# Ten weight blocks of two hybrid layers split by engines instead of by transfers

## The chip, the cores and the metric

The kernel runs on one core of one Trainium2 chip. The metric is the device time of one execution in microseconds. Engines are named as the profile names them: PE (TensorE, with PEld for its weight loads), DVE (VectorE), ACT (ScalarE), POOL (GpSimd) and SP (SyncE, which only issues transfers). Every engine takes its instructions strictly in its own order; an instruction that waits holds up all that stand behind it on that engine.

## The reference, cut to what matters

Two hybrid layers, then one mixer layer with a mixture of experts, over 256 rows of width 1024 in float32. Each layer begins with a norm and one wide product with its input weights; the change touches only how these weights get on the chip in the hybrid layers.

```python
def hybrid_layer(x, norm_g, w_in, conv_w, ...):
    h = rms_norm(x, norm_g)
    z = h @ w_in                        # [256, 1024] @ [1024, 2840]
    (rg_x, rg_gate, q, k_c, v_c, k_s, v_s, k_w, v_w, nsa_gate, br_gate) = jnp.split(z, cuts, axis=-1)
    y_a = rg_lru(causal_depthwise_conv(rg_x, conv_w, conv_b), ...) * jax.nn.silu(rg_gate)
    y_b = nsa(q, k_c, v_c, k_s, v_s, k_w, v_w, br_gate, q_g, k_g, ...) * jax.nn.silu(nsa_gate)
    return x + jnp.concatenate([y_a, y_b], axis=-1) @ w_out

def reference(...):
    for l in range(2):
        x = hybrid_layer(x, norm_g[l], w_in[l], ...)
    return second_block(x, ...)         # mixer layer, then the experts (403 MB of weights)
```

## The kernel before

Products keep float32 accuracy with three passes in a rounded format: each operand is stored as a rounded part `hi` and the rest `lo = src - hi`, and `mm3_steps` (L304) adds hi by hi, lo by hi and hi by lo. So every weight block needs a `hi` and a `lo` before PE can go through its second and third pass.

**Blocks.** The weights of a layer come in blocks of 128 partitions by up to 2048 columns (1 MB). Blocks 0 to 15 belong to hybrid layer 0, 16 to 31 to layer 1, those from 32 on to the mixer. Two blocks make a chunk (half of the 1024 rows each). In a hybrid layer the chunks are, in order: queries (blocks 0, 1), selected and window keys and values (2, 3), compressed keys and gates (4, 5, only 1120 columns each), the recurrent input for the convolution (6, 7), two gates (8 to 11), then the output weights (12 to 15). In layer 1 the same with 16 more. Block i lives, `hi` and `lo` together, in ring room `RING[i % 5]`; a new block can be written there only when PE is done with the block five before it.

**Two ways to split.** For blocks 0 to 3, SP loads the raw float32 block into a room of its own (L254), ACT copies it to `hi` with rounding in four quarters (L277), and POOL and DVE in turn subtract to get the quarters of `lo` (L280). For every other block POOL issues a transfer that rounds into `hi` on the way (L256); when it has landed, ACT writes `-hi` into `lo` (L286, four pieces); then POOL issues two transfers that read the same block again and add it onto `lo` (L291). Such a block is read twice from memory and passes three times through POOL's queue.

**Order.** A scheduler lays out each engine's instructions; the code's order decides what is allocated where. `issue` starts loads one chunk ahead. `step` and `merged` mix the recurrent half (`rg_part`, a generator) with attention. In a layer, PE does the query chunk for both row tiles, the key chunk, the compressed chunk (each as `dense`, whose result the profile calls `mm<-w,hT`), then the convolution's input (`denseT`, `mm<-hT,w`: four groups of 24 products with 256 columns), mixed with attention's transposes (L542, L546), which need the rope of queries and keys on DVE (L532 to L412). The product tiles `mm` have two buffers: PE can't begin a third product before ACT has read the first (L503, L509 and L514, L528 and L529).

**Arena.** All other tiles are ranges of one SBUF tile, the arena, kept by a first-fit allocator (`t`, `region`, `free`). The scheduler makes a writer wait for all earlier users of the same range.

After the mixer come the experts: 192 loads of 2 MB by SP (L1544, L1559) into rooms that PE empties.

Of the kernel before, what the change touches and what calls it, by code (L numbers as in the profile page):

```python
# [36 lines left out]
ARENA = 24512  # L37
BLOCK, NB = 4096, 7
RING = (6, 2, 3, 0, 1)
WS = 2  # L40
AS = 1
HN = 4
# [18 lines left out]
def run_all(steps):  # L61

    while True:
        try:
            next(steps)
        except StopIteration as end:
            return end.value
# [18 lines left out]
class Net:  # L86
# [156 lines left out]
    def issue(self, upto):  # L243

        while self.nload < min(upto, len(self.blocks)):
            name, idx, off, n = self.blocks[self.nload][:4]
            b = self.block(RING[self.nload % 5], "w", F32R, 2)[:, :, :n]
            src = self.A[name][idx][:, off:off + n]
            if self.nload < 4:

                if self.nload % 2 == 0:
                    raw = self.block(5 if self.nload else RING[4], "raw", F32, 2)
                src = raw[:, self.nload % 2, :n]
                self.nc.sync.dma_start(src, self.A[name][idx][:, off:off + n])  # L254
            else:
                self.nc.gpsimd.dma_start(b[:, 0], src)  # L256
            self.loaded.append((b, src))
            self.nload += 1
# [4 lines left out]
    def weights_steps(self, name, k, pin=False):  # L263
# [4 lines left out]
        i = self.ntake  # L268
        b, src = self.loaded[i]
# [1 line left out]
        hi, lo = b[:, 0], b[:, 1]  # L271
        m = hi.shape[-1]
        r = lambda a: a.rearrange("p (k n) -> p k n", k=k)
        if i < 4:
            for q in range(4):
                sl = slice(q * m // 4, (q + 1) * m // 4)
                a = self.S.copy(hi[:, sl], src[:, sl])  # L277
                if pin:
                    self.tc.keep_in_program_order(a)
                (self.V if q % 2 else self.G).tensor_tensor(lo[:, sl], src[:, sl], hi[:, sl].bitcast(F32), OP.subtract)  # L280
                yield 0
            return r(hi), r(lo)
        n = 4 if m > 1024 else 1
        for i in range(n):
# [6 lines left out]
                self.G.dma_start(lo[:, sl], src[:, sl], accum_op=OP.add)  # L291
            yield 0
        return r(hi), r(lo)

    def mm3(self, *a):
        for _ in self.mm3_steps(*a):
# [182 lines left out]
    def hybrid(self, l, w0, then):  # L479
# [6 lines left out]
        keep = set(self.live)  # L486
# [196 lines left out]
        for s in range(10):  # L683
# [28 lines left out]
                        self.split(yt, yB[:, 0, i], yB[:, 1, i], V)  # L712
            step(2 * HD)
        run_all(self.side)
        if then:
            self.norm_start(l + 1)
            keep |= {"xn", "g", "nss"}
        wo = [self.weights("w_out", 2) for i in range(2)]
        w0 = self.chunk(self.blocks[self.ntake][0]) if then else None
        self.out_part(yB, wo, then)  # L720
# [1161 lines left out]
```

## Time and profile before

| what | us |
|---|---|
| median of 3 runs | 1502.34 |
| lowest, highest | 1496.47, 1507.82 |
| profiled execution, its own time | 1497.17 |
| span of the profiled execution, first to last instruction | 1495.5 |
| PE busy in the span | 1204.1 (81%) |
| DVE, ACT, POOL busy | 421.6, 314.4, 149.2 |

The profiled execution took 1.67 us outside its span, and lies 5.2 us below the median. All positions in what follows are microseconds from the start of the span. Layer 0 runs to about 158 us, layer 1 to about 305, the mixer to about 560, the experts to the end. Layer 1's query product begins at 158.45.

### The profile page before, as it was taken

The page shows a single profiled execution, that of the slowest core. Times are in us where ns is not written, and L with a number is a line of the kernel's source. Part 1 is how long each engine was busy: PE and PEld are TensorE (multiplying, and loading weights), DVE is VectorE, ACT ScalarE, POOL GpSimd, SP SyncE. Part 2 cuts the span into 40 slices and gives each one's busy share as a digit, 9 for nine tenths or more (in the row PEclk, how much of TensorE's full clock was granted, in tenths as well). Part 3 has the DMA queues.
Part 4 walks back from the last instruction along what each step waited for, and adds up shares of the span by engine and source line. Part 5 has one row for each costly group of instructions (what it writes and reads, how often), then busy time and mean ns, then how long its engine had stood idle before and what let it go on. Part 6 is the DMA issues. An engine that isn't in the chain of part 4 may idle for free.

```text
span 1495.5 us, 20667 instructions
## 1 busy us (share of the span) xinstructions
PE 1204.1 (81%) x8695; PEld 668.8 (45%) x8695; DVE 421.6 (28%) x1250; ACT 314.4 (21%) x751; POOL 149.2 (10%) x202
## 2 busy tenths in 40 slices
PE   6899889989779998787686786876877868768775
PEld 5777687767657674333132331331322313314311
DVE  5556355636235573110110110110101101101010
ACT  5466457564323321000000000000000000000000
POOL 5222331233213100000000000000000000000000
PEclk9899999989889898898897888997988979888897
DMA  9978998898856479999999999999999999999996
GB/s 332 256 193 189 273 256 228 178 229 207 184 114 171 152 279 365 428 429 426 428 427 428 428 428 428 428 428 428 427 428 428 428 427 427 429 428 427 422 408 231
DMA packets 62149, 510.27 MB, mean 341 GB/s; under 512 B 5708, under 2 KB 5836, under 8 KB 34660
## 3 DMA queue, kind: packets, MB, share of 16 engines
q1 hardware_dynamic: 42180, 418.26, 66.7%
q0 software_dynamic: 19872, 90.65, 25.2%
q8 instruction: 70, 1.15, 0.3%
q14 instruction: 27, 0.22, 0.0%
HBM read 507.83 MB, written 1.05 MB: 340 GB/s over the span
## 4 chain that ended last, share of the span: by engine, by line
PE 37%; DMA 33%; issue 4%; DVE 2%; POOL 2%; ACT 0%; POOLq 0%; DVEq 0%; ACTq 0%
DMA slot<-in_wu 19%; DMA arena<-in_wu 13%; PE sc L1610 10%; PE ot L1641 8%; PE tp L1581 8%; PE mm L304 4%; DMA arena<-in_wd 1%; DMA w<-in_w_in 1%; PE tp L1632 1%; POOL w L291 1%; DVE arena L1628 1%; PE mm L1649 0%; PE ot L1059 0%; PE sc L1376 0%; PE ot L1231 0%
## 5 line engine op out<-in xcount | busy, mean ns | idle before, releaser
L1610 PE MATMUL sc<-slot,arena 128*32 128x512 f32 x1424 | 325.4, 737 | 133.9 <-DMA slot<-in_wu 81.7
L1610 PE MATMUL sc<-arena 128*32 128x512 f32 x624 | 185.9, 733 | 61.2 <-DMA arena<-in_wu 37.6
L1610 PEld LDWEIGHTS sc<-slot,arena 128*32 128x32 f32 x1424 | 69.7, 130 | 308.2 <-issue 121.5
L304 PE MATMUL mm<-hT,w 128*128 128x256 f32 (+1 forms) x936 | 137.8, 301 | 10.9 <-DMA w<-in_w_in 7.2
L304 PEld LDWEIGHTS mm<-hT,w 128*128 128x128 f32 (+1 forms) x936 | 123.3, 200 | 23.9 <-DMA w<-in_w_in 8.4
L1581 PEld LDWEIGHTS tp<-arena 128*128 128x128 f32 x512 | 124.3, 334 | 17.9 <-issue 17.9
L1581 PE MATMUL tp<-arena 128*128 128x128 f32 x512 | 128.5, 406 | 2.4 <-DVE arena L1579 2.4
L1641 PE MATMUL ot<-slot,arena 128*32 128x512 f32 x704 | 124.7, 596 | 2.8 <-DMA slot<-in_wd 2.1
L286 ACT ACTIVATE w<-w 128x512 fp32r<-128x512 f32 (+2 forms) x184 | 99.7, 596 | 73.0 <-DMA w<-in_w_in 45.4
L1610 PEld LDWEIGHTS sc<-arena 128*32 128x32 f32 x624 | 40.5, 130 | 165.9 <-issue 75.9
L304 PE MATMUL mm<-w,hT 128*128 128x512 f32 (+1 forms) x432 | 106.1, 400 | 7.5 <-DVE arena L504 4.5
L304 PEld LDWEIGHTS mm<-w,hT 128*128 128x128 f32 x432 | 79.4, 202 | 24.4 <-issue 6.5
L1627 DVE SCALAR_TENSOR_TENSOR arena<-arena,sc 128x512 f32<-128x512 f32 x16 | 11.0, 688 | 265.8 <-ACT arena L1626 265.8
L1628 DVE SCALAR_TENSOR_TENSOR arena<-arena,sc 128x512 f32<-128x512 f32 x16 | 11.0, 688 | 265.2 <-PE sc L1610 265.2
L1651 DVE TENSOR_TENSOR arena<-arena,mm 128x512 f32<-128x512 f32 x64 | 44.0, 687 | 118.4 <-PE mm L1649 118.4
L1641 PE MATMUL ot<-arena 128*32 128x512 f32 x320 | 71.9, 608 | 3.6 <-DMA arena<-in_wd 3.6
L304 PE MATMUL mm<-w,y 128*128 128x512 f32 x288 | 74.0, 402 | 0.1
L291 POOL DMA_DIRECT2D w<-in_w_in x68 | 61.2, 960 | 119.4 <-ACT w L286 101.9
L1634 ACT COPY arena<-tp 128x512 f32<-128x512 f32 x16 | 9.4, 586 | 302.1 <-PE tp L1632 302.1
L1646 ACT COPY arena<-ot 128x512 f32<-128x512 f32 x32 | 18.8, 586 | 250.5 <-PE ot L1641 250.5
L1649 PE MATMUL mm<-arena 128*128 128x512 f32 x128 | 64.6, 628 | 1.6 <-ACT arena L1646 1.4
L1626 ACT ACTIVATE arena<-sc 128x512 f32<-128x512 f32 x16 | 9.6, 597 | 261.4 <-PE sc L1610 261.4
(386 smaller groups left out, 1226.8 us busy)
## 6 DMA issues: line engine op xcount, KB each, us to landing
slot<-in_wg SPq DMA_DIRECT2D x47, 2048.0 KB, 31.3
slot<-in_wu SPq DMA_DIRECT2D x42, 2048.0 KB, 33.6
slot<-in_wd SPq DMA_DIRECT2D x42, 2048.0 KB, 35.4
arena<-in_wu SPq DMA_DIRECT2D x22, 2048.0 KB, 33.4
arena<-in_wd SPq DMA_DIRECT2D x18, 2048.0 KB, 35.0
arena<-in_wg SPq DMA_DIRECT2D x17, 2048.0 KB, 31.9
w<-in_w_in POOLq DMA_DIRECT2D x28, 1024.0 KB, 7.9
w<-in_w_in POOLq DMA_DIRECT2D x56, 512.0 KB, 8.4
```

Of the source, the lines that this page charges most:

```text
L286: a = self.S.activation(lo[:, sl], hi[:, sl].bitcast(F32), AF.Copy, scale=-1.0)
L291: self.G.dma_start(lo[:, sl], src[:, sl], accum_op=OP.add)
L304: ins = self.T.matmul(out, lhsT=lhs[k][a], rhs=rhs[k][b], start=(first and i == 0 and k == 0), stop=(last and i == 2 and k == n - 1))
L1581: ins = T.matmul(self.rows[k // 4][:, k % 4 * 128:(k % 4 + 1) * 128], lhsT=hv[:, tt, k], rhs=D[:, tt], start=(tt == 0 and k % 4 == 0), sto ...
L1610: T.matmul(dst[32 * j:32 * j + 32], lhsT=XT[:, k, 32 * j:32 * j + 32], rhs=w(j), start=(k == 0), stop=(k == 7))
L1627: V.scalar_tensor_tensor(hid, hid, 1.0, pg, OP.add, OP.mult)
L1628: V.scalar_tensor_tensor(hid, hid, 0.5, pu, OP.mult, OP.mult)
L1632: T.transpose(ps[:, k * 128:(k + 1) * 128], hw[:, k], self.ident)
L1641: T.matmul(py[h][32 * j:32 * j + 32], lhsT=HT[:, k, 32 * j:32 * j + 32], rhs=w(j), start=(k == 0), stop=(k == 3))
L1646: S.copy(Y[:, cs], py[h])
L1649: T.matmul(pc, lhsT=DT[:, tt * 128:(tt + 1) * 128], rhs=Y[:, cs], start=True, stop=True)
L1651: V.tensor_tensor(xs, xs, pc, OP.add)
```

## The change

Blocks 4 to 7 and 16 to 21 (`ENGINES`) are split as blocks 0 to 3 are. Their raw data goes into two rooms in the arena, `raw0` for even blocks and `raw1` for odd ones, 2048 columns each. A room is loaded again when both engines have subtracted from it; `nsplit` counts the blocks split so far and `issue` stops at a block whose room still holds one that isn't. Blocks 8 to 15, 22 to 31 and all of the mixer's stay with the transfers. The tiles of a layer are freed a little earlier in the code, so that the two rooms fit for the next layer's first blocks.

```diff
--- before.py
+++ after.py
@@ -37,6 +37,7 @@
 ARENA = 24512
 BLOCK, NB = 4096, 7
 RING = (6, 2, 3, 0, 1)
+ENGINES = (4, 5, 6, 7, 16, 17, 18, 19, 20, 21)
 WS = 2
 AS = 1
 HN = 4
@@ -244,6 +245,8 @@
 
         while self.nload < min(upto, len(self.blocks)):
             name, idx, off, n = self.blocks[self.nload][:4]
+            if self.nload in ENGINES and self.nload - 2 in ENGINES and self.nload - 2 >= self.nsplit:
+                break
             b = self.block(RING[self.nload % 5], "w", F32R, 2)[:, :, :n]
             src = self.A[name][idx][:, off:off + n]
             if self.nload < 4:
@@ -252,6 +255,12 @@
                     raw = self.block(5 if self.nload else RING[4], "raw", F32, 2)
                 src = raw[:, self.nload % 2, :n]
                 self.nc.sync.dma_start(src, self.A[name][idx][:, off:off + n])
+            elif self.nload in ENGINES:
+
+                name = f"raw{self.nload % 2}"
+                src = (self.view(self.live[name][0], [128, 2048]) if name in self.live else
+                       self.t([128, 2048], name))[:, :n]
+                self.nc.sync.dma_start(src, self.A[self.blocks[self.nload][0]][idx][:, off:off + n])
             else:
                 self.nc.gpsimd.dma_start(b[:, 0], src)
             self.loaded.append((b, src))
@@ -271,7 +280,7 @@
         hi, lo = b[:, 0], b[:, 1]
         m = hi.shape[-1]
         r = lambda a: a.rearrange("p (k n) -> p k n", k=k)
-        if i < 4:
+        if i < 4 or i in ENGINES:
             for q in range(4):
                 sl = slice(q * m // 4, (q + 1) * m // 4)
                 a = self.S.copy(hi[:, sl], src[:, sl])
@@ -279,6 +288,11 @@
                     self.tc.keep_in_program_order(a)
                 (self.V if q % 2 else self.G).tensor_tensor(lo[:, sl], src[:, sl], hi[:, sl].bitcast(F32), OP.subtract)
                 yield 0
+            self.nsplit = i + 1
+            if i in ENGINES:
+                if i + 2 not in ENGINES:
+                    self.free(f"raw{i % 2}")
+                self.issue(self.ntake + 1 + self.ntake % 2)
             return r(hi), r(lo)
         n = 4 if m > 1024 else 1
         for i in range(n):
@@ -291,6 +305,8 @@
                 self.G.dma_start(lo[:, sl], src[:, sl], accum_op=OP.add)
             yield 0
         return r(hi), r(lo)
+
+    nsplit = 0
 
     def mm3(self, *a):
         for _ in self.mm3_steps(*a):
@@ -712,9 +728,10 @@
                         self.split(yt, yB[:, 0, i], yB[:, 1, i], V)
             step(2 * HD)
         run_all(self.side)
+        self.free(*(n for n in list(self.live) if n not in keep))
         if then:
             self.norm_start(l + 1)
-            keep |= {"xn", "g", "nss"}
+            keep |= {"xn", "g", "nss", "raw0", "raw1"}
         wo = [self.weights("w_out", 2) for i in range(2)]
         w0 = self.chunk(self.blocks[self.ntake][0]) if then else None
         self.out_part(yB, wo, then)
```

What moves, by engine. A weight tile is called `w_` and its number in each program; L280 and L277 of before stand as L289 and L286 after, L256, L286 and L291 of before as L265, L300 and L305 after, and L528, L529 (the reads of the compressed chunk's product) as L544, L545.

POOL, from the splits of blocks 2 and 3 on. Before, with blocks 4 and 5 as `w_175` and `w_329`, block 6 as `w_331`, 7 as `w_373`, 8 as `w_375`:

```order
L256 DMA w_175<-in_w_in 128x1120
L280 TENSOR_TENSOR w_74<-raw_75,w_74 128x512 x2
L280 TENSOR_TENSOR w_77<-raw_75,w_77 128x512
L256 DMA w_329<-in_w_in 128x1120
L280 TENSOR_TENSOR w_77<-raw_75,w_77 128x512
L291 DMA w_175<-in_w_in 128x560
L256 DMA w_331<-in_w_in 128x2048
L291 DMA w_175<-in_w_in 128x560
L291 DMA w_329<-in_w_in 128x560 x2
L291 DMA w_331<-in_w_in 128x1024 x2
L256 DMA w_373<-in_w_in 128x2048
L256 DMA w_375<-in_w_in 128x2048
```

After, with blocks 4 and 5 again `w_175` and `w_329`, 6 as `w_339`, 7 as `w_377`, and 8, 9, 10 as `w_379`, `w_455`, `w_457`:

```order
L289 TENSOR_TENSOR w_74<-raw_75,w_74 128x512 x2
L289 TENSOR_TENSOR w_77<-raw_75,w_77 128x512 x2
L289 TENSOR_TENSOR w_175<-arena,w_175 128x280 x2
L289 TENSOR_TENSOR w_329<-arena,w_329 128x280 x2
L265 DMA w_379<-in_w_in 128x2048
L289 TENSOR_TENSOR w_339<-arena,w_339 128x512
L265 DMA w_455<-in_w_in 128x2048
L289 TENSOR_TENSOR w_339<-arena,w_339 128x512
L289 TENSOR_TENSOR w_377<-arena,w_377 128x512 x2
L265 DMA w_457<-in_w_in 128x2048
```

The loads and additions of blocks 4 to 7 are gone from the queue; eight subtractions stand there, and the loads of blocks 8 and 9 stand between and ahead of the subtractions of blocks 6 and 7.

ACT in the same stretch, before; `mm_288` is the key chunk's second product, `mm_346` and `mm_383` are the compressed chunk's two, `w_373` and `w_375` blocks 7 and 8:

```order
L509 ACTIVATE arena<-mm_288 128x256
L514 COPY arena<-mm_288 128x256
L528 COPY arena<-mm_346 128x256
L529 ACTIVATE arena<-mm_346 128x24
L286 ACTIVATE w_373<-w_373 128x512 x4
L528 COPY arena<-mm_383 128x256
L529 ACTIVATE arena<-mm_383 128x24
L286 ACTIVATE w_375<-w_375 128x512 x4
```

And after; `mm_350` and `mm_389` are the compressed chunk's products, `w_339` and `w_377` are blocks 6 and 7, `w_379` and `w_455` blocks 8 and 9:

```order
L530 COPY arena<-mm_288 128x256
L286 CAST w_339<-arena 128x512
L544 COPY arena<-mm_350 128x256
L545 ACTIVATE arena<-mm_350 128x24
L286 CAST w_339<-arena 128x512 x3
L300 ACTIVATE w_379<-w_379 128x512 x2
L544 COPY arena<-mm_389 128x256
L545 ACTIVATE arena<-mm_389 128x24
L286 CAST w_377<-arena 128x512 x4
L300 ACTIVATE w_379<-w_379 128x512 x2
L300 ACTIVATE w_455<-w_455 128x512 x2
L564 COPY arena<-tp_440 128x4x128
```

The read of the second compressed product stood behind block 7's rounding load before; after, it stands behind the one of block 8, and the copies of block 7 stand behind it too.

ACT in layer 1, before; `w_1657` is block 21, `mm_1575` and `mm_1616` are the key chunk's products, `mm_1674` and `mm_1711` the compressed chunk's, `w_1659`, `w_1701` and `w_1703` blocks 22 to 24:

```order
L286 ACTIVATE w_1657<-w_1657 128x280 x3
L509 ACTIVATE arena<-mm_1575 128x256
L286 ACTIVATE w_1657<-w_1657 128x280
L514 COPY arena<-mm_1575 128x256
L286 ACTIVATE w_1659<-w_1659 128x512 x4
L509 ACTIVATE arena<-mm_1616 128x256
L514 COPY arena<-mm_1616 128x256
L528 COPY arena<-mm_1674 128x256
L529 ACTIVATE arena<-mm_1674 128x24
L286 ACTIVATE w_1701<-w_1701 128x512 x4
L528 COPY arena<-mm_1711 128x256
L529 ACTIVATE arena<-mm_1711 128x24
```

And after, with `mm_1591`, `mm_1632`, `mm_1694`, `mm_1731` for the same products and `w_1675`, `w_1721`, `w_1723` for blocks 22 to 24:

```order
L525 ACTIVATE arena<-mm_1591 128x256
L300 ACTIVATE w_1675<-w_1675 128x512 x2
L530 COPY arena<-mm_1591 128x256
L300 ACTIVATE w_1675<-w_1675 128x512 x2
L525 ACTIVATE arena<-mm_1632 128x256
L530 COPY arena<-mm_1632 128x256
L300 ACTIVATE w_1721<-w_1721 128x512
L544 COPY arena<-mm_1694 128x256
L545 ACTIVATE arena<-mm_1694 128x24
L300 ACTIVATE w_1721<-w_1721 128x512 x3
L300 ACTIVATE w_1723<-w_1723 128x512
L544 COPY arena<-mm_1731 128x256
```

The reads of `mm_1694` and `mm_1731` stand behind a piece of block 23 and of block 24 now; before, only the second stood behind such a piece, of block 23.

## Rows read from the trace of the kernel before

**Rows 1.** Windows: busy us (instructions) of PE, PEld, DVE, ACT, POOL; clock, DMA share, GB/s.
```profile
45.00:62.00 17.00, 10.10 (x56) 9.01 (x56) 5.06 (x14) 6.15 (x13) 4.68 (x6) 0.70 0.97 301
62.00:158.40 96.40, 94.84 (x668) 73.85 (x669) 59.77 (x227) 64.40 (x170) 23.31 (x33) 1.00 0.84 201
158.40:207.20 48.80, 40.63 (x188) 33.47 (x187) 16.67 (x50) 19.13 (x43) 16.85 (x22) 0.86 1.04 275
...
560.00:1495.50 935.50, 705.90 (x3819) 276.15 (x3819) 127.66 (x300) 46.14 (x88) 0.58 (x1) 0.85 0.99 416
```

**Rows 2.** Timeline, 18 to 28.5 us: start, duration, engine, line, operation, [idle before].
```profile
19.40 0.78 POOL L256 DMA_DIRECT2D w<-in_w_in  x1 [1.19 <-DVE w L280]
20.19 3.82 POOL L280 TENSOR_TENSOR w<-raw,w 128x512 fp32r<-128x512 f32 x3
...
22.04 4.35 DVE L280 TENSOR_TENSOR w<-raw,w 128x512 fp32r<-128x512 f32 x1 [2.08 <-ACT w L277]
...
27.87 0.94 PE L304 MATMUL mm<-w,hT 128*128 128x512 f32 x3 [2.54 <-DVE arena L504]
```

**Rows 3.** Timeline of PE, 45 to 62 us.
```profile
45.08 0.86 PE L304 MATMUL mm<-hT,w 128*128 128x256 f32 x6
...
51.40 1.22 PE L304 MATMUL mm<-hT,w 128*128 128x256 f32 x4 [1.88 <-ACT arena L529]
55.70 1.01 PE L304 MATMUL mm<-hT,w 128*128 128x256 f32 x3 [3.08 <-DMA w<-in_w_in]
...
57.64 4.21 PE L304 MATMUL mm<-hT,w 128*128 128x256 f32 x24
61.93 0.63 PE L542 MATMUL tp<-arena 128*128 128x128 f32 x4
```

**Rows 4.** Timeline of PE, 163 to 208 us.
```profile
163.41 7.31 PE L304 MATMUL mm<-w,hT 128*128 128x512 f32 x31
172.65 4.14 PE L304 MATMUL mm<-w,hT 128*128 128x512 f32 x10 [1.93 <-DVE arena L504]
...
182.37 13.99 PE L304 MATMUL mm<-w,hT 128*128 128x512 f32 x74 [1.80 <-DMA w<-in_w_in]
...
201.04 1.01 PE L304 MATMUL mm<-hT,w 128*128 128x256 f32 x3 [2.02 <-DMA w<-in_w_in]
...
207.30 0.60 PE L542 MATMUL tp<-arena 128*128 128x128 f32 x4
```

**Rows 5.** Line L291 (accumulating transfers), 168.5 to 171.8 us.
```profile
L291 POOL DMA_DIRECT2D w<-in_w_in x4: 856/875/920, 168.6 to 171.7; - x4
...
DMA to landing us min/median/max: 6.2/8.4/10.5
```

**Rows 6.** Line L254 (raw loads by SP), whole span.
```profile
L254 SPq DMA_DIRECT2D raw<-in_w_in x4: 432/459/478, 2.2 to 3.7; - x4
...
DMA to landing us min/median/max: 7.4/9.4/13.4
```

**Rows 7.** Line L256 (rounding loads), 145 to 146 us: one load.
```profile
DMA to landing us min/median/max: 5.6/5.6/5.6
```

**Rows 8.** Line L256, 40 to 41.4 us: two loads.
```profile
DMA to landing us min/median/max: 8.6/9.6/10.5
```

**Rows 9.** Line L256, 172 to 173.2 us: two loads.
```profile
DMA to landing us min/median/max: 11.4/12.5/13.5
```

**Rows 10.** Timeline of DVE, 50 to 54 us: the rope of the first row tile.
```profile
51.48 0.95 DVE L536 TENSOR_TENSOR arena<-arena 128x768 f32<-128x768 f32 x1
...
53.20 0.36 DVE L412 TENSOR_TENSOR arena<-arena 128x192 f32<-128x192 f32 x1
```

**Rows 11.** Groups by line: shapes xcount | busy us, mean ns | idle before.
```profile
L286 ACT ACTIVATE w<-w 128x512 fp32r<-128x512 f32 (+2 forms) x184 | 99.7, 596 | 73.0 <-DMA w<-in_w_in 45.4 <-issue 17.9 <-DMA w<-in_w_out 9.7
...
L280 POOL TENSOR_TENSOR w<-raw,w 128x512 fp32r<-128x512 f32 x8 | 11.7, 1485 | 2.2 <-ACT w L277 2.2
```

**Rows 12.** Line L280 on DVE, whole span: ns min/median/max, when.
```profile
L280 DVE TENSOR_TENSOR w<-raw,w x8: 677/681/4349, 12.1 to 26.4; 128x512 fp32r<-128x512 f32 x8
```


## The prediction

> **What bounds the kernel now.** I read the windows first [rows 1], to see which stretch has time to give. From 560 us on the transfers are busy 99% of the time at 416 GB/s: the experts are bound by memory, and the change doesn't touch them; they only start earlier if what is ahead of them ends earlier. Between 62 and 158 us PE is busy for 94.8 of 96.4 us at full clock: nothing to gain there, but what is gained ahead of it is carried through. Two windows are different. From 45 to 62 us PE is busy for 10.1 of 17 us, at a granted clock of 0.70; from 158.4 to 207.2 for 40.6 of 48.8 us at 0.86, while the transfers are busy all the time (1.04). These are the beginnings of the two hybrid layers, where the blocks in question are used. What ends PE's waits there is in its timelines: transfers of weights (3.08 us in layer 0; 1.80 and 2.02 us in layer 1), and reads of the product tiles by ACT and DVE that stood behind such a transfer (1.88 and 1.93 us) [rows 3, 4]. So transfers of weights bound these two stretches, directly or through ACT's queue.
>
> **What a block costs the transfers.** Four additions of half a block each were issued from 168.6 to 171.7 us and landed 6.2 to 10.5 us later [rows 5]: from 174.8 to 182.2, so 7.4 us for three more, 2.5 us each. Four raw loads of a whole block, issued from 2.2 to 3.7 us, landed from 9.6 to 17.1 [rows 6]: also 2.5 us each. Half a block that is added takes as long as a whole one that is only loaded. A full block thus goes from 2.5 + 2 x 2.5 = 7.5 us of transfers to 2.5, with one latency in place of two in a row. For six full blocks that is 30 us of transfers less, and four of about half the size save some 11 more. That is no gain by itself; the gain is what PE waits less.
>
> **Part A, the first splits (layer 0, 22 to 28 us).** PE waited 2.54 us for DVE's read of the first product, which stood behind a subtraction that took 4.35 us while POOL subtracted for blocks 2 and 3 [rows 2]. In POOL's queue the load of block 4 stood ahead of these (a wait of 1.19 us, then 0.78 us to issue), that of block 5 between them. Both leave POOL. I take 1.3 us; the bounds are 0 (DVE remains as slow) and 2.5 (the whole wait).
>
> **Part B, layer 0, 45 to 62 us.** From the convolution's first product (45.08) to the transposes of the second row tile (61.93) are 16.85 us, in which PE does 47 products of 256 columns (37 in the rows shown, 10 between them) and 6 transposes. At the 0.86 us for 6 that the first row shows, the products are 6.7 us; transposes at 0.63 for 4 are 0.9 [rows 3]. So 9.2 us are waits and half clock. After the change blocks 6 and 7 come raw, early, and PE has block 6 when it needs it. A new wait stands on ACT: the read of the second compressed product and the copies of block 7 are behind block 8's load. That can be issued when the key chunk is done, about 39 us (it was 40.1 behind other work), and nothing else is then on the queues; the nearest row is a load alone, 5.6 us to landing [rows 7], the far one is 8.6 us [rows 8]. With 5.6 it lands at 44.7; two pieces of ACT (0.6 us each [rows 11]) and the reads end at 46.5; the rope takes 2.1 us [rows 10] plus two of DVE's subtractions between its steps, 1.4, so the first transposes start at 50.0, and the second after these (0.9) and 24 products (3.4), at 54.3. That is 7.6 us earlier. Bounds: 4.6 with the far row, 9.2 if nothing waits. I take 7.
>
> **Part C, layer 1, 158 to 207 us.** From the query product (158.45) to the transposes of the second row tile (207.30) are 48.85 us. The work is 96 products of 512 columns at 7.31/31 = 0.236 us, 22.7; 48 of 280 columns, out of the 74 in 13.99 us (26 of which are wide: 6.1), 7.9; 29 of 256 columns, 4.2; 14 transposes, 2.2 [rows 3, 4]. Sum 37.0, so 11.9 us are lost. After the change blocks 16 to 21 no longer pass POOL's queue of transfers, and the waits for the key chunk go. Late next are blocks 22 and 23, which still do. Block 22's room is free when the query product ends (170.7 [rows 4]); its load stands behind POOL's subtractions for blocks 18 to 20 (six of 1.5 us at most [rows 11], two of them half as long), about 174. Alone it lands in 5.6 us [rows 7], at 179.6; before, it took 11.4 to 13.5 there [rows 9]. After two pieces of ACT its first addition is issued at 181 and lands at 186.5; block 23's load, block 24's, block 22's second addition and block 23's two follow at 2.5 us each: 189, 191.5, 194, 196.5, 199. PE ends the compressed chunk near 190 and waits for them; with 12 products after the last (1.7 us) the second transposes stand at 200.7, and by the order 19 more products are done by then than before (2.7 us). That is 9.3 us. Ahead of the layer the four subtractions for blocks 16 and 17 stand on POOL before the norm's power, which PE's transposes wait for; this may cost 1 us. Bounds: 3 (block 22 lands as late after its issue as before, 5.8 us more) and 11.9. I take 8.
>
> **Hidden parts.** ACT does as many pieces per block as before. DVE gets 20 subtractions, of 0.7 us each in the middle [rows 12]; it was busy for a third of these two windows [rows 1], so I cost them at nothing but the 1.4 us above and 0.5 us in part C. If that cover is missing, the second rival below holds. POOL loses three issues per block and gets two subtractions, an even trade. The two rooms take free ranges of the arena; their loads in layer 1 wait for attention's last readers, 14 us ahead of the query product, and a raw block needs some 5 us and its split 3.
>
> **Sum.** 1.3 + 7 + 8 - 0.5 = 15.8, about 16 us. Against the profiled execution's 1497.2 that is 1481. That execution lies 5.2 us below the median of 1502.3, so the median forecast is 1502.3 - 16 = 1486.
>
> **Rivals.**
> *The wait moves to the blocks that stay with the transfers.* ACT's queue stands still until block 8, and in layer 1 pieces of 22 to 24, have landed, and the reads of PE's product tiles are behind them. For it: the order, and that such a read was already the end of two of PE's waits [rows 3, 4]. Against it: these loads find empty queues now. With the landings of [rows 8, 9], parts A to C give 0 + 4 + 3, less 1: 6 us, a median of 1496.
> *POOL holds DVE.* One subtraction of DVE took 4.35 us while POOL subtracted [rows 2], six times the median of 0.68 [rows 12]; POOL's own mean is 1.5 us [rows 11]. Each of the 20 new POOL subtractions can hold up a DVE step that PE waits for (rope, norm, reads of products) by 1.5 us: 30 us at most, and slower than before by 14, a median of 1516. It decides from where more than 11 of the 20 stand in PE's way. Against it: at least half of the eight took 0.68 us or less, though POOL subtracted in the same stretch [rows 12], and most of the 20 fall where PE works on blocks that are ready. The Trainium skill (SBUF — State Buffer, Who interferes with whom) states the rule behind this: a DVE instruction with two SBUF inputs and a GpSimd instruction that reads SBUF exclude each other, and the later one waits for the whole of the other. By that rule the change puts on two engines that exclude each other what the transfers did beside them; the 4.35 us agree with it.
> *Nothing arrives.* If the experts' stream started by something other than PE's progress, both layers could end earlier at no gain: 1502. Against it: their rooms are freed by PE and by the layers' tiles.
>
> **How the numbers follow.** A measurement of this kernel can tell about 1%, 15 us, from no change. Forecast 0.62, the moved wait 0.22, POOL holding DVE 0.08, nothing arriving 0.08. The forecast's parts run from 10 to 22 us, and some seven tenths of it lie over 15 us: faster 0.45. The rest of it, the moved wait and most of the last case are within 1%: 0.47. Slower: 0.08. The range takes the forecast and the moved wait, with the 4 us by which a median of such runs can be off: 1479 to 1500.
>
> **What the profile after would show.** Right: PE's window that begins with the convolution of layer 0 at a clock over 0.9; the transposes of its second row tile 6 to 9 us earlier; layer 1's another 5 to 9; the key chunk of layer 1 without waits; loads of block 8 and 22 landing in under 7 us; 30 to 40 us less of transfers between 25 and 220 us. Wrong: a wait of ACT for block 8 or 22 of over 5 us with PE idle behind it; subtractions of DVE with a mean over 2 us and PE's waits ended by DVE; or both layers earlier and the first expert product not.

## The result, and the profile after

The changed kernel takes 1490.62 us (median of 11 runs, 1489.62 to 1495.42); the kernel before, on the same chip, 1502.69 (median of 11, 1496.47 to 1507.82). The ratio is 0.993, with a 95% interval of 0.9914 to 0.9946: 12.1 us by the medians, 10.5 by the ratio. The profiled execution after took 1491.46 us, with a span of 1489.8.

The windows of two stretches, with the columns of [rows 1]:

```profile
45.00:62.00 17.00, 14.11 (x93) 12.63 (x94) 14.05 (x32) 12.69 (x28) 8.80 (x9) 0.90 0.81 203
...
158.40:207.20 48.80, 43.14 (x292) 37.49 (x291) 31.66 (x76) 26.65 (x60) 20.15 (x22) 0.93 0.79 208
```

Against [rows 1], PE is busy for 14.1 of 17 us in place of 10.1, the clock rose from 0.70 to 0.90, and the transfers' share fell from 0.97 to 0.81; in layer 1 it is 0.93 in place of 0.86, and 0.79 in place of 1.04. DVE is busy for 14.1 us of these 17, up from 5.1. The timeline of PE after, in layer 0, answers to [rows 2, 3]:

```profile
26.61 17.36 PE L320 MATMUL mm<-w,hT 128*128 128x512 f32 x96 [0.67 <-ACT arena L519]
...
45.37 2.63 PE L320 MATMUL mm<-hT,w 128*128 128x256 f32 x17 [0.70 <-ACT arena L545]
...
49.30 0.38 PE L320 MATMUL mm<-hT,w 128*128 128x256 f32 x1 [0.74 <-POOL w L289]
50.72 0.66 PE L558 MATMUL tp<-arena 128*128 128x128 f32 x4 [1.04 <-DVE arena L428]
...
55.82 0.60 PE L558 MATMUL tp<-arena 128*128 128x128 f32 x4
```

The stretch that began at 27.87 begins at 26.61, and the transposes of the second row tile (61.93) stand at 55.82. No wait for a weight transfer is left; the longest is 1.04 us, for DVE's rope. The same for the end of layer 0 and for layer 1, beside [rows 4]:

```profile
123.53 0.96 PE L320 MATMUL mm<-w,y 128*128 128x512 f32 x3
...
151.51 0.63 PE L364 MATMUL tp<-arena 128*128 128x128 f32 x4 [1.62 <-DVE arena L361]
...
152.89 3.40 PE L320 MATMUL mm<-w,hT 128*128 128x512 f32 x14
...
166.91 17.39 PE L320 MATMUL mm<-w,hT 128*128 128x512 f32 x96 [1.32 <-DVE arena L520]
185.37 0.98 PE L320 MATMUL mm<-hT,w 128*128 128x256 f32 x6 [1.07 <-ACT arena L545]
189.04 4.30 PE L320 MATMUL mm<-hT,w 128*128 128x256 f32 x17 [2.69 <-ACT arena L545]
...
197.22 0.63 PE L558 MATMUL tp<-arena 128*128 128x128 f32 x4
```

Layer 0's first output product starts at 123.53 (before: 130.81), so 7.3 us are in hand. PE then waits for DVE at 151.5 (the norm) and at 166.9 (the read of a product), and at the key chunk, where 172.65 became 166.91, 5.7 are left. The second row tile's transposes of layer 1 come 10.1 us earlier (197.22 against 207.30), ACT being what PE waited for last. The query product, at 158.45 before, begins at 152.89. ACT's timeline shows for what it waited itself:

```profile
184.33 0.63 ACT L300 ACTIVATE w<-w 128x512 fp32r<-128x512 f32 x1 [4.94 <-DMA w<-in_w_in]
184.87 0.35 ACT L544 COPY arena<-mm 128x256 f32<-128x256 f32 x1
...
188.00 0.63 ACT L300 ACTIVATE w<-w 128x512 fp32r<-128x512 f32 x1 [1.13 <-DMA w<-in_w_in]
188.54 0.35 ACT L544 COPY arena<-mm 128x256 f32<-128x256 f32 x1
```

ACT waits 4.94 us for the load of block 23, then 1.13 for block 24's, with a read of a compressed product right behind each. What reaches the end is read at the first product of the experts, after and (second line, a trace of the kernel before) before:

```profile
566.77 3.64 PE L1627 MATMUL sc<-arena 128*32 128x512 f32 x32
```

```profile
575.91 3.64 PE L1610 MATMUL sc<-arena 128*32 128x512 f32 x32
```

The difference is 9.1 us. From there on the two traces run alike: the last output has landed at 1490.98 before and 1481.97 after, 9.0 apart. But the spans differ by 5.7 only, since the end of the program became longer (below, among the surprises).

### The profile page after: what moved, and what is told of

The parts are those of the page before. It is cut to its first block, busy times and chain, and to the rows that moved or that the text cites. A ratio compares the mean times of both kernels' runs of the same rounds, so it can differ in the third digit from the quotient of the medians.

```text
span 1489.8 us, 20684 instructions
## 1 busy us (share of the span) xinstructions
PE 1200.4 (81%) x8695; PEld 669.1 (45%) x8695; DVE 447.1 (30%) x1270; ACT 315.5 (21%) x751; POOL 151.8 (10%) x192
## 4 chain that ended last, share of the span: by engine, by line
PE 45%; DMA 37%; issue 8%; DVE 5%; POOL 3%; ACT 2%; POOLq 0%; ACTq 0%; DVEq 0%; SPq 0%
DMA slot<-in_wu 19%; DMA arena<-in_wu 13%; PE sc L1627 10%; PE ot L1658 8%; PE mm L320 8%; PE tp L1598 8%; DMA w<-in_w_in 3%; POOL w L305 1%; PE sc L705 1%; PE tp L841 1%; DMA arena<-in_wd 1%; PE tp L1649 1%; PE ot L719 1%; DVE arena L1645 1%; ACT w L300 1%
## 5 line engine op out<-in xcount | busy, mean ns | idle before, releaser
L1627 PE MATMUL sc<-arena 128*32 128x512 f32 x624 | 185.4, 727 | 63.3 <-DMA arena<-in_wu 38.4
L300 ACT ACTIVATE w<-w 128x512 fp32r<-128x512 f32 (+1 forms) x144 | 81.0, 612 | 50.9 <-DMA w<-in_w_in 19.7
L1658 PEld LDWEIGHTS ot<-slot,arena 128*32 128x32 f32 x704 | 33.2, 109 | 64.3 <-issue 56.1
## 6 DMA issues: line engine op xcount, KB each, us to landing
arena<-in_wg SPq DMA_DIRECT2D x17, 2048.0 KB, 31.3
```

Source lines behind the costliest of these rows:

```text
L300: a = self.S.activation(lo[:, sl], hi[:, sl].bitcast(F32), AF.Copy, scale=-1.0)
L1627: T.matmul(dst[32 * j:32 * j + 32], lhsT=XT[:, k, 32 * j:32 * j + 32], rhs=w(j), start=(k == 0), stop=(k == 7))
L1658: T.matmul(py[h][32 * j:32 * j + 32], lhsT=HT[:, k, 32 * j:32 * j + 32], rhs=w(j), start=(k == 0), stop=(k == 3))
```

## The experiments

Positions in the traces, in us; "traced" is the profiled execution's own time, the last column the median of the timed runs. Layer 0 (L0) and layer 1 (L1) by the second row tile's first transposes and by the first output product.

| kernel | L0 transposes | L0 output | L1 transposes | L1 output | first expert product | traced | median |
|---|---|---|---|---|---|---|---|
| before | 61.9 | 130.8 | 207.3 | 277.4 | 575.9 | 1497.2 | 1502.7 |
| before_2 | 66.1 | 135.0 | 211.7 | 281.8 | 579.7 | 1499.6 | |
| after | 55.8 | 123.5 | 197.2 | 266.4 | 566.8 | 1491.5 | 1490.6 |
| l0_only | 55.5 | 123.5 | 204.0 | 273.9 | 572.7 | 1494.4 | 1495.9 |
| l1_only | 66.4 | 135.3 | 212.4 | 281.2 | 586.2 | 1506.3 | 1501.7 |
| act_order | 54.2 | 125.9 | 197.5 | 273.9 | 574.6 | 1498.8 | 1497.1 |
| sub_dve | 54.0 | 119.7 | 189.6 | 258.3 | 557.1 | 1481.4 | 1491.5 |
| sub_dve_2 | 53.8 | 119.4 | 187.9 | 256.6 | 559.7 | 1484.6 | 1490.8 |
| sub_dve_3 | 53.7 | 131.4 | 200.6 | 269.3 | 570.1 | 1495.1 | |
| more22 | 54.3 | 125.8 | 199.9 | 279.1 | 585.3 | 1509.9 | 1504.9 |
| more22_dve | 53.9 | 119.6 | 185.1 | 267.1 | 569.4 | 1494.7 | 1499.8 |
| more22_sq | 53.6 | 128.8 | 194.3 | 262.0 | 565.0 | 1487.4 | 1492.5 |
| sub_dve_sq | 54.1 | 129.7 | 198.4 | 267.1 | 572.6 | 1498.0 | 1492.2 |
| eng11 | 53.7 | 130.6 | 200.4 | 269.1 | 571.6 | 1495.8 | 1493.4 |

Measured beside the variants, the kernel before had medians of 1502.2, 1503.2, 1502.9 and 1504.3; each ratio below is against the one beside it.

### Each layer alone: l0_only and l1_only

```diff
-ENGINES = (4, 5, 6, 7, 16, 17, 18, 19, 20, 21)
+ENGINES = (4, 5, 6, 7)                      # l0_only
+ENGINES = (16, 17, 18, 19, 20, 21)          # l1_only
```

> Only blocks 4 to 7 (layer 0) are split by engines; layer 1 goes by transfers as before. Theory (each layer's gain is its own and is carried through): layer 0's first output product stands at about 123.5 us as after the whole change (130.8 before), layer 1's loss of 1.5 us ahead of its key chunk is not there, and the first expert product comes at 575.9 - 7.3 = 568.6, a time 7 us under before. Rival (layer 1's blocks by transfers take the gain of layer 0 back, since their loads wait on PE and queue the same way wherever they start): no more than 3 us, first expert product at 573.

> Only blocks 16 to 21 (layer 1) are split by engines; layer 0 as before. Theory: layer 0's output product stays at 130.8 us, the second row tile's transposes of layer 1 come 4.5 us before the 207.3 of before, and the first expert product at about 573 to 574, 2 to 3 us earlier; both halves add up to the 9.1 us of the whole change. Rival (the two halves need each other: layer 1 gains the 8 us of the prediction by itself): first expert product at 568.

l0_only: ratio 0.9961 (0.9938 to 0.9984), 6.3 us by the medians. l1_only: 0.9984 (0.9965 to 1.0003), 0.4 us by the medians, 2.4 by the ratio, and not clear of zero. Together that is 6.7 to 8.3, against 12.1 or 10.5 for the whole: most of it is layer 0, and the halves add up to the whole only roughly, within these intervals. The trace of l0_only has something of both of its readings:

```profile
123.47 0.96 PE L320 MATMUL mm<-w,y 128*128 128x512 f32 x3 [0.20 <-DVE arena L766]
...
155.83 1.09 PE L364 MATMUL tp<-arena 128*128 128x128 f32 x4 [6.65 <-DVE arena L361]
```

Layer 0's output product stands where it does after the whole change, and then PE waits 6.65 us for the norm ahead of layer 1. By the medians the theory's 7 us is nearly there; against the trace of before at 575.9, the first expert product at 572.7 is the rival's number. The two go together because that trace is one of before's quick executions, which the next run shows. The rival's reason is not what the trace shows. Block 16's load was issued 7.3 us sooner than before (138.35 against 145.61), but took 12.5 us to land where it took 5.6 [rows 7]. Ahead of it stands a transfer of 2 MB by SP, the compression weights of layer 1, which the kernel before issued at 163.06 (the second line is that of block 16's load):

```profile
136.84 0.33 SPq L539 DMA_DIRECT2D arena<-in_w_cmp  x1
...
DMA to landing us min/median/max: 12.5/12.5/12.5
```

That this transfer is what holds the load up is read from the order, and was not tested. In the changed kernel it is issued at 138.63, behind the raw loads of blocks 16 and 17 (136.78).

The trace of l1_only fits neither of its readings: its first expert product is at 586.2, where 573 and 568 were expected. Layer 0's output product is at 135.3, where before_2 below has it too, and not at 130.8. From there to the second transposes of layer 1 it is 77.1 us (before 76.5): 6.6 us are gained from the query product on, but 7.1 lost ahead of it, where PE waits 1.08 and 2.89 us for DVE. Another 6.5 us are lost between layer 1's output product and the experts. This trace is of the slowest of its twelve executions.

### The kernel before, traced again: before_2

> The kernel before, once more, for a second trace. Its times spread from 1495.7 to 1512.1 us, and in two traces in which layer 0 has the same program the load of block 6 took 7.5 and 9.8 us to land. Theory (the spread comes from how soon the transfers of the two layers land): span differences appear before the first expert product, which comes later than 575.9 by what the run is longer, and from there to the last product of PE it is 910 to 911 us as in both traces. Rival (the experts' stream varies): first expert product within 1 us of 575.9, and the difference after it.

The same program came to the second row tile 4.2 us later. The load of block 6 in the two traces, before and before_2:

```profile
L256 POOL DMA_DIRECT2D w<-in_w_in x1: 868/868/868, 29.0 to 29.0; - x1
...
DMA to landing us min/median/max: 7.5/7.5/7.5
```

```profile
L256 POOL DMA_DIRECT2D w<-in_w_in x1: 863/863/863, 28.9 to 28.9; - x1
...
DMA to landing us min/median/max: 9.7/9.7/9.7
```

It lands 2.2 us later after its issue, and the additions behind it follow. The first expert product is 3.8 us later, and from there to PE's last product it is 910.6 and 908.5 us, so the experts give back 2.1. So the theory holds for the larger part: in this pair the layers differ by more than the experts do, though its 910 to 911 us are not met. Against this second trace the changed kernel's first expert product is 12.9 us earlier. The gain of 9.1 us read from the first pair is therefore at the low side of what the medians hold.

### The subtractions off POOL: sub_dve, three times

```diff
-                (self.V if q % 2 else self.G).tensor_tensor(lo[:, sl], src[:, sl], ...)
+                (self.V if q % 2 or i in ENGINES else self.G).tensor_tensor(lo[:, sl], src[:, sl], ...)
```

> The subtractions of blocks 4 to 7 and 16 to 21 all go to DVE, none to POOL: 40 in place of 20 on DVE, and POOL reads no SBUF beside them. Theory (DVE and POOL hold each other up, which is why a DVE subtraction takes 1.37 us in the middle): DVE's subtractions of 512 columns fall to about 0.68 us, DVE's steps of one row of small tiles to 0.2 us, layer 1's loss of 1.5 us ahead of its key chunk goes, and the first expert product comes 2 to 3 us before the changed kernel's 566.8. Rival (twice the subtractions on a busy DVE are the price, 0.68 us each, and the two engines don't hold each other): DVE's subtractions keep 1.3 us and the first expert product is 2 to 4 us later.

> The kernel with all subtractions on DVE, once more: its twelve times spread from 1480 to 1499 us with a median of 1491.5, the same as the changed kernel's 1490.6, though the profiled execution, at 1481.4, had its first expert product 9.7 us earlier. Theory (the profiled one was lucky in its transfers; the others lose in the same waits for blocks 8, 22 and 23): a second trace near 1491 has the same durations of DVE (0.68 us) and loses some 10 us behind transfers in the two layers. Rival (the time is lost in the mixer or the experts' stream): first expert product at 557 again, and a longer rest.

> The kernel with all subtractions on DVE a third time, for a trace of one of its slower executions (12 of 20 were over 1489 us; the two traced ones were at 1481 and 1485). Theory: a trace over 1489 has a stretch of half clock of some 20 us in the attention of one of the layers behind a wait of PE of 2 to 3 us that the fast traces don't have. Rival: such a trace is slower in the mixer or in the experts, or shows longer transfers without a fall of the clock.

The line of DVE's subtractions in layer 1 (ns: min/median/max), in the changed kernel and in sub_dve, first two fences, and of a small step of DVE in the changed kernel's layer 0, third:

```profile
L289 DVE TENSOR_TENSOR w<-arena,w x8: 750/1207/1785, 159.8 to 170.8; 128x512 fp32r<-128x512 f32 x4, 128x280 fp32r<-128x280 f32 x4
```

```profile
L289 DVE TENSOR_TENSOR w<-arena,w x16: 443/566/686, 153.4 to 162.8; 128x512 fp32r<-128x512 f32 x8, 128x280 fp32r<-128x280 f32 x8
```

```profile
L335 DVE TENSOR_SCALAR arena<-arena x2: 173/670/1167, 36.4 to 39.9; 128x12 int32<-128x12 int32 x2
```

With POOL beside it, a DVE subtraction takes up to 1.79 us here (1.98 in layer 0), without POOL never more than 0.69, at twice as many. The step of 128 x 12 elements takes 0.17 us and once 1.17, when it began 0.15 us after a subtraction of POOL did and ended with it. Steps that read one operand from PSUM are not touched: two residual sums (L416, at 142.23 and 145.59) lie wholly beside subtractions of POOL and take 0.69 and 0.67 us, and without POOL in the kernel before the same sums take 0.69. So the theory of the hold is right, and the waits of 1.62 and 1.32 us ahead of layer 1's key chunk are gone. In two traces the first expert product comes 9.7 and 7.1 us ahead of the changed kernel's, far more than the 2 to 3 expected. The scheduler also orders PE's work otherwise here, so not all of that is the hold alone.

And yet the median is the same: ratios 0.9923 (0.99 to 0.9947) and 0.9921 (0.989 to 0.9952), times from 1480 to 1499. The second trace, at 1484.6, is a quick one again and decides nothing between its readings. The third, at 1495.1, shows what one of the slower executions loses. ACT in layer 0, in sub_dve_2 and then in sub_dve_3:

```profile
66.97 0.63 ACT L300 ACTIVATE w<-w 128x512 fp32r<-128x512 f32 x1 [1.42 <-DMA w<-in_w_in]
67.62 0.38 ACT L765 ACTIVATE arena<-mm 128x256 f32<-128x256 f32 x1
67.90 0.25 ACT L630 ACTIVATE arena<-tp 15x128 f32<-15x128 f32 x1
```

```profile
68.44 0.63 ACT L300 ACTIVATE w<-w 128x512 fp32r<-128x512 f32 x1 [2.98 <-DMA w<-in_w_in]
69.10 0.38 ACT L765 ACTIVATE arena<-mm 128x256 f32<-128x256 f32 x1
69.38 0.25 ACT L630 ACTIVATE arena<-tp 15x128 f32<-15x128 f32 x1
```

One load, block 11's, has landed 1.47 us later. The reads behind it on ACT (L765 of a product, L630 of the compressed keys) come 1.48 later, and PE, which waited 0.74 us once in sub_dve_2, waits twice:

```profile
69.99 1.09 PE L320 MATMUL mm<-hT,w 128*128 128x256 f32 x7 [0.75 <-DVE arena L766]
72.39 0.28 PE L641 MATMUL tp<-arena 15*128 15x15 f32 x1 [1.30 <-DVE arena L428]
```

From there the granted clock is at the lower of its two levels, 1.2 GHz, for 24 us. Windows of PE, sub_dve_2 first (busy us, instructions, clock, DMA share, GB/s):

```profile
72.00:96.00 24.00, 24.00 (x163) 1.00 0.76 168
```

```profile
72.00:96.00 24.00, 23.61 (x86) 0.51 0.52 98
96.00:120.00 24.00, 24.00 (x178) 0.99 0.53 145
```

In the same 24 us, with PE busy for all but 0.4 of them, 86 matmuls are done in place of 163. Layer 0's output product is at 131.4 in place of 119.4: 12 us, behind 1.5 us of a transfer. This is the theory of the third trace, with waits of 0.75 and 1.30 us. The mean clock of the timed runs fits it, with some overlap: it is 0.883 to 0.893 in the eight under 1487 and 0.877 to 0.886 in the twelve above.

### Order on ACT: act_order

```diff
+LATE = (23, 24)
...
-            if pin:
+            if pin or self.ntake - 1 in LATE:
                 self.tc.keep_in_program_order(a)
```

> As changed, but ACT reads both compressed products of layer 1 before any negation of blocks 23 and 24. Theory of the wait on ACT (what PE lost in layer 1 is that these reads stood behind the loads of blocks 23 and 24, PE waits of 1.07 and 2.69 us there): second row tile's transposes 3 us before the changed kernel's 197.2, first expert product 2 to 3 us before 566.8. Rival (the blocks themselves come late: PE needs the added halves of 22 and 23, which land from 180.8 to 195.3): PE waits as long, behind transfers instead, within 1 us of 566.8 or later.

Ratio 0.9962 (0.9945 to 0.9979), some 6 us behind the changed kernel by the medians. The time is the rival's. Two rows of PE:

```profile
191.17 2.48 PE L320 MATMUL mm<-hT,w 128*128 128x256 f32 x12 [3.04 <-DMA w<-in_w_in]
...
216.60 1.43 PE L320 MATMUL mm<-hT,w 128*128 128x256 f32 x5 [3.14 <-DMA w<-in_w_in]
```

The wait went from ACT to the transfer (3.04 us), the second transposes stayed (197.5), and since block 24's negations had moved back as well, PE later waited 3.14 us for it. After this second wait the clock stands at 0.50 from 216 to 229 us, and the output product is 7.5 us later than in the changed kernel, 2.4 of them from layer 0 of this trace. Counted from its own key chunk (169.35, against 166.91 in the changed kernel) the second transposes do come 2.1 us sooner, part of the theory's 3 us, and the delay of block 24 loses more. So the order on ACT is not the whole of the loss in layer 1: with the reads freed, PE waits for the landing of block 22's second addition instead. How much of the loss is the order and how much the landing, this run does not separate, since it moved block 24 as well.

### Two more blocks by engines: more22, more22_dve

```diff
-ENGINES = (4, 5, 6, 7, 16, 17, 18, 19, 20, 21)
+ENGINES = (4, 5, 6, 7, 16, 17, 18, 19, 20, 21, 22, 23)
```

> As changed, and blocks 22 and 23 are split by engines too. Theory (what is left in layer 1 is these two blocks' double passage through POOL's queue, directly and through the reads on ACT behind them): the PE waits of 1.07 and 2.69 us at 185 to 189 go, the second row tile's transposes come at about 192 to 193 in place of 197.2, and the time falls by 3 to 4 us. Rival (the wait moves on to blocks 24 and 25, three pieces of which now stand ahead of the second compressed product's read): within 1 us of the changed kernel.

> As the run before it (blocks 22 and 23 by engines too), with all subtractions of these blocks on DVE. Theory (POOL's subtractions hold DVE and the norm's power up, and the transfers that are left wait for nothing then): 2 to 3 us better than with half of them on POOL. Rival (24 more subtractions on DVE cost what the lock costs): the same time.

Both expectations failed. more22: ratio 1.0022 (1.0003 to 1.0041), 14 us behind the changed kernel; more22_dve 0.9983 (0.996 to 1.0005). In more22_dve the second row tile's transposes are at 185.1, 12 us ahead of the changed kernel, as the theory wants, and still the output product comes no earlier (267.1 against 266.4). Its ACT, its PE, and PE's windows:

```profile
200.90 0.63 ACT L300 ACTIVATE w<-w 128x512 fp32r<-128x512 f32 x1 [3.49 <-DMA w<-in_w_in]
201.55 0.27 ACT L630 ACTIVATE arena<-tp 15x128 f32<-15x128 f32 x1
```

```profile
204.62 0.23 PE L641 MATMUL tp<-arena 15*128 15x15 f32 x1 [2.94 <-DVE arena L428]
```

```profile
205.00:229.00 24.00, 23.75 (x87) 0.50 0.57 110
229.00:245.00 16.00, 15.76 (x115) 1.00 0.41 133
```

The wait moved on, not to blocks 24 and 25 but to block 27: ACT stood 3.49 us for its load, the compressed keys' square (L630) behind it, PE without work for 2.94 us, and then 24 us at half clock with PE busy: the 12 us. more22 has the same after a wait of 1.98 us (clock 0.64 from 212 to 240), and its second transposes, at 199.9, are not even early.

### Taking that one wait away: more22_sq, sub_dve_sq, eng11

```diff
-                S.activation(sq[0:15], pcv, AF.Square)
+                V.tensor_copy(sq[0:15], pcv); V.tensor_tensor(sq[0:15], sq[0:15], sq[0:15], OP.mult)
...
+ENGINES = (4, 5, 6, 7, 11, 16, 17, 18, 19, 20, 21)     # eng11: sub_dve and block 11
```

> As the kernel with blocks 22 and 23 by engines and all subtractions on DVE, but the square of the compressed keys' norm is taken by DVE (a copy and a product of 15 x 128) in place of ACT, where it stood behind a negation of block 27 whose load landed 8.8 us after its issue. Theory (that wait on ACT left PE without work for 2.94 us ahead of the compressed keys' transposes, and from there to 229 us the granted clock stood at 0.50; the half clock, not the wait, is the 12 us by which 22 and 23 made things worse): PE's wait there falls under 1 us, the clock from 205 to 230 us is 1.0, the first output product of layer 1 comes at about 255 in place of 267.1, and the median falls by some 10 us to 1488 to 1490. Rival (the attention stretch is slow for another reason, such as the later blocks' transfers): the median stays within 3 us of 1499.8.

> As the kernel with all subtractions on DVE (blocks 22 and 23 by transfers), with the same square on DVE. Its times lie from 1480 to 1499 us, with the mean clock at 0.887 to 0.893 below 1486 and at 0.877 to 0.885 above 1492. Theory (the upper ones are executions in which this wait on ACT behind a block that landed late let the clock fall in the attention stretch): with the square off ACT most times lie at 1480 to 1487, median 1485. Rival (the clock falls at another wait, or the other reads on ACT in that chain, which stay, are enough): the spread and the median of 1491 stay.

> As the kernel with all subtractions on DVE, and block 11 is split by engines too. In its slow trace block 11's load landed at 68.4 us against 67.0 in a fast one; ACT's first negation of it stands ahead of the reads from which DVE and PE go on, PE was idle for 0.75 and 1.30 us in place of 0.74, and from 72 to 96 us the granted clock stood at 0.50. Now no block that comes by transfers stands ahead of these reads. Theory (the late landing, by way of the half clock, is the slow mode of 1490 to 1499 us): layer 0 keeps full clock from 72 to 100 us, its first output product comes at about 119.5 in every trace, and the times lie at 1480 to 1487 with a median of about 1484. Rival (the clock falls in layer 0 whatever is ahead on ACT, or in another place): the median stays at 1490 to 1492 and the spread at 15 us or more.

more22_sq: ratio 0.9937 (0.9914 to 0.9961), 1492.5 in place of 1499.8. In its trace PE waits 0.48 us ahead of the compressed keys' transposes of layer 1, the clock from 200 to 240 us is 1.00, and the way from the transposes to the output product, 82.0 us in more22_dve, is 67.7. So in layer 1 it is as the theory says; the output product itself is at 262.0, not 255, because layer 0 fell to half clock this time (0.57 from 72 to 96 us), and the median is above the 1488 to 1490 expected.

sub_dve_sq: 0.9926 (0.9893 to 0.9958), 1480.9 to 1498.0: the rival. Another read (L765) stays behind block 11's negation, and its trace has 0.57 from 72 to 96 us.

eng11: 0.9897 (0.9865 to 0.993), 1482.8 to 1495.8, median 1493.4: the rival again. What was aimed at is reached and does not help. ACT, then PE, in layer 0:

```profile
65.84 0.39 ACT L765 ACTIVATE arena<-mm 128x256 f32<-128x256 f32 x1 [0.43 <-PE mm L320]
66.23 0.27 ACT L630 ACTIVATE arena<-tp 15x128 f32<-15x128 f32 x1
70.88 1.67 ACT L300 ACTIVATE w<-w 128x512 fp32r<-128x512 f32 x3 [4.38 <-DMA w<-in_w_out]
72.45 0.18 ACT L616 ACTIVATE arena<-tp 128x30 f32<-128x30 f32 x1
```

```profile
69.14 0.23 PE L641 MATMUL tp<-arena 15*128 15x15 f32 x1 [0.42 <-DVE arena L428]
...
73.47 1.09 PE L649 MATMUL tp<-arena 128*128 128x64 f32 x4 [2.04 <-DVE arena L645]
```

L765 and L630 wait for no block now, and PE's wait ahead of the compressed keys is 0.42 us. But the next read in the chain, L616, stands behind block 12's load (4.38 us), PE waits 2.04 us one step later, and from 74 to 92 us the clock is 0.50. None of the variants is shown to be faster than the changed kernel: their intervals overlap with 0.9914 to 0.9946.

## Why the prediction was right

The time of 1490.6 lies in the range of 1479 to 1500, between the forecast (1486) and the first rival (1496); the change was clear, though under 1% (0.7%), where the prediction took 1% as the least that could be told. Point by point:

- **Part A**, 1.3 us: measured 1.26 (27.87 to 26.61).
- **Part B**, 7 us: block 8 was issued at 38.4 and landed at 43.7, where 39 and 44.7 were estimated, and ACT's queue held PE up for only 0.70 us. The second transposes came 6.1 us earlier, 4.85 of them after part A, the output product 7.3, or 6.0 after part A. DVE took 0.7 us of the rest: the first transposes are at 50.7, where 50.0 was worked out with 0.7 us for a subtraction; in sub_dve, where it takes that, they are at 50.0. Between the first and the second transposes the clock took more. The second are at 55.8, where 54.3 was worked out, and the granted clock from 50.5 to 56 us is 0.69; act_order and more22, which split the same blocks of layer 0 and have nearly the same waits there, have 1.00, and the second transposes at 54.2 and 54.3. The 24 products between, in the changed kernel and then in act_order:

```profile
51.44 4.54 PE L320 MATMUL mm<-hT,w 128*128 128x256 f32 x24
```

```profile
51.06 3.11 PE L320 MATMUL mm<-hT,w 128*128 128x256 f32 x24
```

- **Part C**, 8 us, is the term that was mis-sized. From layer 0's output product on, the second transposes gained 2.8 us more and the output product 3.7, of which 1.9 were given back ahead of the experts. Counted as the prediction counted, from the query product (158.45, after 152.89), the second transposes came 4.5 us sooner (48.85 to 44.33) where 6.6 were worked out, and the output product 5.4 (118.96 to 113.52) where the 19 products done ahead were to make it 9.3; 1.7 us had been lost ahead of the query product (7.28 to 5.56). The landings were estimated well: block 22's load came 20.8 us after the query product (21.2 estimated), block 23's 31.3 (30.6), block 23's second addition 42.4 (40.6). So the transposes miss the estimate by about what this last addition is late, and of the 2.7 us for the 19 products 0.9 is seen. Meanwhile ACT waited 4.94 us for block 23, PE 1.07 and 2.69 behind it, and the clock was 0.53 from 189 to 195. That is the first rival's mechanism, at 23 and 24; at 8 and 9 it cost 0.70 us. act_order shows that PE waits for the landing too when the reads are freed.
- **POOL and DVE**: the cost "at nothing but 1.4 and 0.5 us" was too low. Ahead of layer 1's key chunk 1.5 us were lost in place of 1 (7.28 to 5.74), and sub_dve's quick traces are 7 to 10 us ahead. The rule of the Trainium skill (SBUF — State Buffer, Who interferes with whom) agrees with the 1.79 against 0.69 us. The 4.35 us that the prediction counted for it are more than the whole of one subtraction of POOL (up to 1.83 in that trace): that step of DVE began at 22.04 and ended at 26.39, past three subtractions of POOL, the last of them from 24.54 to 25.83. No subtraction of DVE took more than 1.98 in the changed kernel. The price of the second rival was real, but nowhere near 30 us, since PE had ready blocks beside most of it.
- **Nothing arrives**: no; the first expert product follows the layers, though not exactly. From layer 1's output product to it the fourteen traces take 297.9 to 306.2 us, a spread that the prediction put at nothing and that no run here explains.
- **The signs named**: the landings of blocks 8 and 22 (5.3 and 5.1 us) and 33 us less of transfers between 25 and 220 us (a share of 0.93 to 0.76) came; layer 1's transposes another 5 to 9 us earlier did not (4.0).

By the traces the parts sum to 9.1 us at the first expert product (12.9 against before_2) where 16 were forecast, and 3.3 us of it are lost again at the end of the program. The median's 12.1 are more than that pair of traces shows, because the profiled execution of before was 5.5 us under its median. The two profiled executions themselves are 5.7 us apart; that the median falls midway between the forecast and the first rival is in that part luck, which no term of the prediction names. That the transfers taken out also take their spread along (nine of the eleven runs after lie within 1.9 us) fits with before_2, but was not tested by itself, and sub_dve, with the same transfers, spreads over 18 us.

What stays open: where the changed kernel loses against sub_dve between 55.8 and 123.5 us (2 us more) beside the changed order; why the clock fell behind the first transposes of layer 0 in the changed kernel and not in act_order, after nearly the same waits; and why after the wait of 2.69 us in the changed kernel the clock was back at 195 us and after 2.94 us in more22_dve only at 229, with PE busy nearly all the time after both.

## What to carry to other kernels

A split that an engine can do beside its other work can be worth more than a transfer that sums, when the queue is what PE waits for: it was for these ten blocks, and not for 22 and 23 on top of them. Price it with the engines as they share SBUF, here 1.8 us in place of 0.7. Before an order is tuned, look for reads of products that stand behind something that waits for a transfer: when the wait is taken away it moves to the next block that still comes so (23, 27, 11 and 12 here). And cost a wait of PE by what the granted clock does after it, not by its length, and look at several executions, since in one pair of them a landing 1.5 us later stood ahead of a loss of 12 us.

## What the runs showed of the hardware that was not expected

- **A short wait, a long half clock.** PE waits of 0.75 and 1.30, 2.04, 2.94 and 3.14 us were followed by 13 to 24 us at 0.50 to 0.51, in stretches in which PE was busy for over 95% of the time; a single wait of 0.74 us in the same place was followed by full clock. The length alone does not decide: in the trace of more22_sq a wait of 1.23 us in layer 0 was followed by half clock (0.57 from 72 to 96 us), and waits of 1.23 and 0.48 us in layer 1 by full clock.
- **A step of one small operand can wait for POOL as well**: 0.17 us became 1.17 beside a subtraction of POOL. The Trainium skill (SBUF — State Buffer, Who interferes with whom) names tensor_scalar, which this step is, among the operations that can take the shared ports; this one execution of it agrees.
- **The end of the program changes with the transfers POOL issued.** The drain of POOL after the last output, before and after (ns: min/median/max):

```profile
L1879 POOLq DRAIN  x3: 40/103/1822, 1491.8 to 1495.2; - x3
```

```profile
L1896 POOLq DRAIN  x3: 40/103/6272, 1482.6 to 1489.4; - x3
```

1.82 us with 138 transfers of POOL and 6.27 with 108; 3.41 with 126, 2.92 with 120, 6.03 with 105, 5.78 with 102. It is the same in every trace of one program, and within 102 to 108 and 120 to 126 it grows by 0.08 us for each transfer. Why it steps in between is open. It costs the changed kernel 3.3 us that no engine's work shows.
